# The second block's gates and recurrence inputs by seven block products, its values first and through HBM

## The chip, the cores and the metric

The kernel runs on one core of a Trainium2 chip. The core has five engines with instruction lines of their own: PE (TensorE, the matrix engine), DVE (VectorE), ACT (ScalarE), POOL (GpSimd) and SP (SyncE, which here only starts transfers). Each line is worked off in order. Operands lie in SBUF (128 partitions), matmul results in PSUM (eight banks of 128 x 512 float32), everything else in HBM. The metric is the device time of one execution in microseconds (us), the median of several runs.

## The reference: two blocks over 512 tokens

The input is 512 tokens of 2048 features, in float32. A first block (16 extra tokens, a projection to queries, keys, values and gates of two kinds of attention, an output projection) leaves its result `h`, 512 x 2048. The change is in the second block:

```
xn = rmsnorm_2(h, norm_gain)
proj = xn @ w_in                                  # 2048 -> 6 x 1024
q, k, v, g_sb, x_lru, g_lru = split(proj)
y_sb  = stick_breaking_attention(norm(q), norm(k), v) * silu(g_sb)
xc    = causal_depthwise_conv(x_lru, conv_w, conv_b)     # 4 taps
y_lru = rg_lru(xc, w_a, b_a, w_x, b_x, lam) * silu(g_lru)
h = h + concat(y_sb, y_lru) @ w_out
```

`rg_lru` is a gated recurrence along the tokens, `h_t = a_t h_{t-1} + sqrt(1 - a_t^2) (i_t x_t)`, in eight blocks of 128 channels; its gates come from small 128 x 128 products of `xc`. The gates `g_sb`, `g_lru` and the input `x_lru` are three products of 512 x 2048 by 2048 x 1024; in the kernel they are called GS, GL and XL, eight blocks of 128 columns each. The projection's 2048 input features are sixteen K tiles of 128.

## The kernel before

**Matmuls.** A float32 operand is split into two parts of a shorter format, a rounded one and the rest (`split`, lines 416 to 418: ACT rounds, DVE subtracts). A product is three passes over the parts, large by large, large by rest, rest by large; so each K tile costs three matmuls. `big` holds the split activations of all tokens, features on partitions.

**Two ways of using weights.** `fm` produces features on partitions (lhs is a weight tile, the tokens stream through: up to 512 columns). `tm` produces tokens on partitions (lhs is a tile of 128 tokens, 512 weight columns stream). Both take weight tiles of 128 x 1024 from `load_next` (SP loads to `wraw`, then a split into `wsp`, three buffers, two tiles ahead, in the order of the list `_sequence`).

**Seven products.** The first block's gates and second attention do not take the plain way. Two blocks of 128 feature columns (a pair) times two halves of the tokens times two halves of the first 12 K tiles is a 2 x 2 by 2 x 2 block product, which the function `seven` does with seven block products in place of eight, from sums of the weights and of the activations; the other 4 K tiles are plain (`rest`). The activation sums are formed once (`side_x`: `x23`, `x1s`, and a fourth one that overwrites a part of `big` when its old content is used up). The weight sums are formed for each pair: `load_raw` brings the four quarters into four slots of `wraw` (SP), `sum_up` adds further quarters to them with accumulating transfers (issued by POOL), and `produce` splits each sum into one of four slots of `wsp`. A slot is filled again as soon as its product is done: one of them holds the matrices of products 4, 3 and 7 in turn. Results are recombined by DVE from the four banks (`p1s`, `us`, `wv`, `ts`). There are 20 such pairs in the first block.

**The second block.** `side_pair` finishes `h` for a pair of token tiles: it scales, adds, stores to HBM (`h1d`), transposes on PE and splits into `big`. Then PE goes through XL (`fm`, eight blocks for each half of the tokens, 256 columns at a time), GL and GS (`fm`, 512 columns), and `tm` products for v, q and k, and the output projection (O2). The results of XL, GL and GS stay in SBUF in `ybuf`, sixteen slots. `side_lru` does the recurrence for a block once its XL is there; `sb_scores` and `sb_sums` do the eight attention heads, between q, k and O2 matmuls.

**What sets the order.** `main_work` yields after small groups of matmuls; a driver (`run`) puts steps of the side generators between them, by an estimate of when their inputs are ready. PE's order is the order of that program. The order on DVE, ACT, POOL and SP is set by `Plan`: it records every instruction, gives it a due time from the PE instructions that need it, and lists each engine's work by due time, with fixed costs per instruction and per byte of a transfer.

Of the kernel before, what the change touches and what calls it, by code (L numbers as in the profile page):

```python
# [46 lines left out]
def _units():  # L47
# [6 lines left out]
    for name, n in (("KA", 2), ("VA", 2), ("GA", 8), ("QB", 8), ("KB", 8), ("VB", 8), ("GB", 8)):  # L54
        for i in range(n):
            if name in ("KA", "VA"):
                u[(name, i)] = ("fm", 0, i, cols)
            SEVEN_COLS[(name, i)] = cols
            cols += P
# [11 lines left out]
    for name in ("GS", "XL", "GL"):  # L71
        for i in range(8):
            u[(name, i)] = ("fm", 2, i, cols)
            cols += P
# [6 lines left out]
QK_LAST = (0, 2, 3, 1)  # L81


def _pairs():

    pairs = [(("GA", i), ("GA", i + 1)) for i in range(0, 8, 2)] + [(("GB", i), ("GB", i + 1)) for i in range(0, 8, 2)]
    for h in range(0, 8, 2):
        pairs += [(("QB", h), ("KB", h)), (("VB", h), ("VB", h + 1)), (("QB", h + 1), ("KB", h + 1))]
    return pairs


PAIRS = _pairs()


def _sequence():
# [5 lines left out]
    seq += [("XL", b) for _ in range(2) for b in range(8)]  # L101
    seq += [("GL", b) for b in range(8)] + [("GS", b) for b in range(8)]
    for c in range(4):
        if c % 2 == 0:
            seq += [("v", c // 2, kg) for kg in range(4)]
        seq += [("qk", c, kg) for kg in (QK_LAST if c == 3 else range(4))]
    seq += [("O2", n, kg) for n in range(4) for kg in (0, 2, 3)] + [("O2", n, 1) for n in range(4)]
# [3 lines left out]
class Plan:  # L111
# [9 lines left out]
    def __init__(self):  # L121
        self.ins, self.engine, self.cost, self.busy, self.func, self.preds = [], [], [], [], [], []
        self.nbytes = []
# [54 lines left out]
    def __call__(self, ins):  # L178
# [50 lines left out]
        self.nbytes.append(0)  # L229
        if op == "DMACopy":  # L230
# [21 lines left out]
    def order(self):  # L252
# [36 lines left out]
        while count < N:  # L289
# [60 lines left out]
def hybrid_two_block_kernel(ctx: ExitStack, tc: tile.TileContext, wp, wq, wc, xT, xtok, par, lvec, cst, rg, pg, lruw, out):  # L350
# [183 lines left out]
    ybuf = Later(lambda: next_turn([("ybuf", [P, KT, NTOK], F32)])[0])  # L534
    ar = T([P, 6144], "ar")
# [14 lines left out]
    qd = dram.tile([NT, P, NTOK], F32, tag="qd", name="qd")  # L550

# [26 lines left out]
    taken = [0]  # L578
    barred = [seq.index((("VA", 1), 1)) + 1]
# [17 lines left out]

    def load_raw(p, r, slot):
        if p >= len(PAIRS):
# [7 lines left out]
    def sum_up(p, r, q):  # L607

        pool.dma_start(pair_raw[(p, r)], wq[p, q], accum_op=ALU.add)  # L609

    def produce(p, i):


        if p >= len(PAIRS):
# [22 lines left out]
        elif i == 6:  # L637
            w_slots[:] = [at["a"], at["d"], at["c"], at["b"]]
            load_raw(p + 1, 0, raw_slot[(p, 4)])
        elif i == 8:  # L640
            load_raw(p + 1, 1, raw_slot[(p, 5)])
            if p + 1 < len(PAIRS):
                sum_up(p + 1, 1, 2)
        elif i == 7:
            load_raw(p + 1, 2, raw_slot[(p, 2)])
        elif i == 9:
            load_raw(p + 1, 3, raw_slot[(p, 0)])
# [36 lines left out]
    def seven(p, r, c0a, c0b, evac_a1, evac_b, evac_a2, after=None):  # L684


        cs = (c0a, c0b)
        X1, X2 = slice(0, HL), slice(HL, L)

# [33 lines left out]
        produce(p + 1, 1)  # L723
# [4 lines left out]
        if p == 0:  # L728
            yield when("x4")
        yield from product(7, 1, lambda xs, j: big[:, xs, j, HL + c0b : L], slice(c0b, HL), True, False)  # L730
        produce(p + 1, 4)
# [5 lines left out]
        produce(p + 1, 2)  # L737
        yield from product(9, 3, lambda xs, j: big[:, xs, KS + j, X2], allc, False, True)
        yield from evac_a2()
        produce(p + 1, 5)  # L740
# [4 lines left out]
    def tm(units, x0, evac, kgs=range(4), toks=range(NT), before_unit=None, after_unit=None, chore=None):  # L745
# [3 lines left out]
        for i, unit in enumerate(units):  # L749
# [5 lines left out]
            if last:  # L755
# [5 lines left out]
            for n, (t, h) in enumerate(order):  # L761
                if chore and n % 2:
                    chore()
                if last:
# [9 lines left out]
                if last and n % 4 == 3:  # L774
                    yield from evac({k: accs[k] for k in (t - 1, t)})
            if after_unit:
                after_unit(kg)
        post("calm", 2500)
# [76 lines left out]
    def silu2(g_ps, rb, dst):  # L855
        g, th = et(512), et(512)
        dve.tensor_tensor(g, g_ps, rb, ALU.mult)
        ins = act.activation(th, g, AF.Tanh, scale=0.5).ins
        dve.scalar_tensor_tensor(dst, th, 1.0, g, op0=ALU.add, op1=ALU.mult)
        return ins  # L860

    def gate_y(slot, hf, o):
        y = ybuf[:, slot, hf * 256 : (hf + 1) * 256]
        dve.scalar_tensor_tensor(y, o, 0.5, y, op0=ALU.mult, op1=ALU.mult)

    def split_y(s):
        split(big[:, 0, s, :NTOK], big[:, 1, s, :NTOK], ybuf[:, s, :])
# [16 lines left out]
    def side_x():  # L884
# [26 lines left out]
        post("x4")  # L911
# [326 lines left out]
    def side_pair(p):  # L1238
# [10 lines left out]
        for i, t in enumerate(toks):  # L1249
            y = yt[:, t, :]  # L1250
            c = slice(t * P, (t + 1) * P)
            for k8 in range(2):
# [7 lines left out]
                xg = T([P, 8, P], "pt")  # L1260
                dve.tensor_tensor(xg, tp, g2[:, kts].unsqueeze(2).broadcast_to([P, 8, P]), ALU.mult)
                post("pss", 2500)
# [598 lines left out]
```

## Time and profile before

| | us |
|---|---|
| median of 3 runs (1707.7 to 1710.82) | 1708.71 |
| the profiled execution, its time | 1711.61 |
| the profiled execution, its span from first to last instruction | 1709.8 |
| PE busy | 1682.0 (98%) |
| DVE busy | 1107.2 (65%) |
| ACT busy | 900.4 (53%) |
| POOL busy | 148.8 (9%) |

Durations in the argument come from the one profiled execution; its time stands 2.9 us above the median of the runs. In the trace's stretches the first block's pairs lie about 161 to 729 us after the start, the output projection of the first block up to 929, XL up to about 1026, GL and GS up to 1213, v, q, k and the output projection with the heads from there on. A row of a group reads: line, engine, operation, tile written <- tiles read, shapes, count, busy time and mean duration of one in ns, then the engine's idle time ahead of it and what ended that.

### The profile page before, as it was taken

What the parts mean: (1) busy time and instruction counts of PE and PEld (TensorE: products, weight loads), DVE (VectorE), ACT (ScalarE), POOL (GpSimd) and SP (SyncE); (2) the same over time, 40 slices, a digit from 0 to 9 for tenths busy, and PEclk for the clock granted to TensorE, in tenths of its full rate; (3) what the DMA queues carried; (4) which work ended last, traced back from release to release, by engine and by line L of the source; (5) the groups of instructions that cost most, each with busy time, mean ns of one, the idle gap of its engine ahead of it and who ended that gap; (6) DMA issues with size and microseconds to landing.
All of it is one profiled execution on the core that took longest, in us unless ns stands there. A gap on an engine that the chain in (4) does not pass through costs nothing.

```text
span 1709.8 us, 26464 instructions
## 1 busy us (share of the span) xinstructions
PE 1682.0 (98%) x10288; PEld 1497.2 (88%) x10288; DVE 1107.2 (65%) x1861; ACT 900.4 (53%) x1493; POOL 148.8 (9%) x165
## 2 busy tenths in 40 slices
PE   8999999999999999999999999999999999999999
PEld 8779999999999999978888998888888888888887
DVE  4684697766799989883567769733223764676433
ACT  5554466664577767674454558722223654564311
POOL 0011122111212222200000001100000000000000
PEclk9999999999999999999999999999999999999999
DMA  7534767667666566553566653223323222432233
GB/s 277 188 126 126 194 157 162 163 160 163 162 136 151 135 144 137 130 189 111 190 215 235 219 186 104 87 95 99 93 92 99 75 66 95 148 112 80 81 94 128
DMA packets 85549, 239.58 MB, mean 140 GB/s; under 512 B 9632, under 2 KB 15392, under 8 KB 83744
## 3 DMA queue, kind: packets, MB, share of 16 engines
q1 hardware_dynamic: 73904, 206.43, 37.1%
q0 software_dynamic: 11520, 31.46, 11.5%
q8 instruction: 81, 1.33, 0.3%
q14 instruction: 44, 0.36, 0.1%
HBM read 220.03 MB, written 17.83 MB: 139 GB/s over the span
## 4 chain that ended last, share of the span: by engine, by line
PE 67%; DVE 4%; DMA 1%; ACT 1%; issue 1%; ACTq 0%; POOLq 0%; DVEq 0%; SPq 0%
PE pj L450 60%; PE pmt L450 2%; PE pss L450 2%; DMA wraw<-in_wq 1%; DVE wsp L418 1%; PE ptt L453 1%; PE bank L450 1%; PE pmt L453 1%; PE pss L453 1%; ACT wsp L417 1%; DVE e L1175 1%; DVE ar L1223 0%; DVE e L1191 0%; ACT e L1190 0%; DVE pt L418 0%
## 5 line engine op out<-in xcount | busy, mean ns | idle before, releaser
L450 PE MATMUL pj<-wsp,big 128*128 128x512 f32 x3072 | 734.5, 396 | 3.0 <-ACT wsp L417 1.0
L450 PEld LDWEIGHTS pj<-wsp,big 128*128 128x128 f32 x3072 | 571.7, 188 | 133.3 <-DVE big L418 1.6
L418 DVE TENSOR_TENSOR wsp<-wraw,wsp 128x1024 fp32r<-128x1024 f32 (+3 forms) x399 | 427.5, 1074 | 342.2 <-ACT wsp L417 336.2
L450 PE MATMUL pj<-big,wsp 128*128 128x264 f32 (+3 forms) x4320 | 635.3, 304 | 10.0 <-ACT wsp L417 7.2
L450 PEld LDWEIGHTS pj<-big,wsp 128*128 128x128 f32 x4320 | 582.5, 189 | 45.7 <-ACT wsp L417 7.5
L417 ACT CAST wsp<-wraw 128x1024 fp32r<-128x1024 f32 (+3 forms) x399 | 367.3, 923 | 444.5 <-PE pj L450 353.4
L609 POOL DMA_DIRECT2D wraw<-in_wq x80 | 70.3, 891 | 409.7 <-DVE wsp L418 242.0
L450 PE MATMUL pj<-x,wsp 128*128 128x264 f32 x720 | 100.8, 286 | 1.9 <-DVE wsp L418 1.9
L450 PEld LDWEIGHTS pj<-x,wsp 128*128 128x128 f32 x720 | 92.5, 188 | 3.0 <-DVE wsp L418 2.7
L417 ACT CAST pt<-ptt 128x512 fp32r<-128x512 f32 (+2 forms) x96 | 50.7, 528 | 50.0 <-PE ptt L453 48.5
L418 DVE TENSOR_TENSOR pt<-ptt,pt 128x512 fp32r<-128x512 f32 (+2 forms) x96 | 59.5, 620 | 24.5 <-ACT pt L417 24.1
L450 PE MATMUL pss<-kk,qq 128*128 128x264 f32 x448 | 72.1, 289 | 2.8 <-DVE vtail L946 1.9
L450 PE MATMUL pmt<-pt,vv 128*128 128x256 f32 (+1 forms) x528 | 69.7, 280 | 2.1 <-DVE ptail L972 2.0
L450 PEld LDWEIGHTS pmt<-pt,vv 128*128 128x128 f32 x528 | 67.1, 188 | 4.5 <-issue 2.0
L1178 ACT ACTIVATE e<-e,sm 128x528 f32<-128x528 f32 x64 | 47.1, 736 | 39.1 <-DVE sm L1175 38.9
L450 PEld LDWEIGHTS pss<-kk,qq 128*128 128x128 f32 x448 | 61.4, 188 | 5.4 <-PE ptt L453 2.6
L1383 POOL TENSOR_SCALAR_AFFINE_SELECT e<-e 128x128 f32<-128x128 f32 x32 | 12.1, 378 | 478.2 <-ACT e L1382 460.8
L453 PE MATMUL ptt<-ident,e 128*128 128x128 f32 x336 | 52.5, 273 | 0.0
L450 PE MATMUL pj<-x1s,wsp 128*128 128x264 f32 x360 | 50.1, 286 | 0.0
L1175 DVE CUSTOM_DVE_ANT_0 e<-pss,ar 128x528 f32<-128x528 f32 x64 | 44.8, 700 | 3.4 <-PE pss L450 3.3
L450 PEld LDWEIGHTS pj<-x1s,wsp 128*128 128x128 f32 x360 | 46.2, 188 | 0.2
L453 PEld LDWEIGHTS ptt<-ident,e 128*128 128x128 f32 x336 | 39.8, 140 | 2.6
(254 smaller groups left out, 1386.4 us busy)
## 6 DMA issues: line engine op xcount, KB each, us to landing
wraw<-in_wp SPq DMA_DIRECT2D x215, 512.0 KB, 3.5
wraw<-in_wq SPq DMA_DIRECT2D x80, 384.0 KB, 4.0
wraw<-in_wq POOLq DMA_DIRECT2D x80, 384.0 KB, 5.1
wraw<-in_wc SPq DMA_DIRECT2D x40, 256.0 KB, 3.2
e<-in_xT SPq DMA_DIRECT2D x28, 264.0 KB, 4.3
early<-in_xtok SPq DMA_DIRECT2D x4, 1024.0 KB, 7.8
gated<-e SPq DMA_DIRECT2D x16, 256.0 KB, 3.7
e<-yd SPq DMA_DIRECT2D x16, 256.0 KB, 4.1
```

Source lines behind the costliest of these rows:

```text
L417: act.copy(hi, src)
L418: dve.tensor_tensor(lo, src, f(hi), ALU.subtract)
L450: _queue(nc.tensor.matmul(out, lhsT, rhs, start=start, stop=stop).ins, cost)
L453: _queue(nc.tensor.transpose(out, in_, identity).ins, 110.0)
L609: pool.dma_start(pair_raw[(p, r)], wq[p, q], accum_op=ALU.add)
L1175: dve.tensor_tensor_reduce(out=halves(x), in0=s[:, :, :HL], in1=halves(bias[:, b0 : b0 + L]), scale=1.0, scalar=3e38, op0=ALU.add, op1=ALU ...
L1178: act.activation(x, x, AF.Exp, scale=-1.0, bias=nm, accum_out=l[:, m : m + 1])
L1383: pool.affine_select(z[:, t * P : w], z[:, t * P : w], [[-1, P]], ALU.is_gt, -1e30, base=0, channel_multiplier=1)
```

## The change

XL, GL and GS are computed by `seven` too, in twelve pairs of blocks, over the first 12 of the 16 K tiles, with the two halves of 256 tokens as token halves. The order is XL and GL pairs in turn, four of each, and then four GS pairs (`SECOND`).

The v products come first, ahead of the pairs: `v_half` does them for the first two token tiles as soon as these are there, and then for the other two, so each v weight tile is loaded twice, as XL's were. The values are scaled by ACT and stored to HBM (`vd`) by POOL. `side_pair` also stores the gained features of each token tile to HBM (`x2d`, POOL); `side_x2` reads them back by K tile (POOL, twelve reads) and DVE forms the operand sums. Where an accumulating transfer would add the weight quarter 2, DVE adds it (`sum_up`), so two of the four accumulating transfers of a pair are left in the second block.

The operands need the room of `ybuf`. So the gates go to HBM (`gated2`) instead; XL has two buffers (`xls`), which the convolution empties; the recurrence's result is multiplied with its gate after a load from `gated2`, and stored there. After the last pair one tile is rebuilt (`ybuf2`): GS's eight gates and the values are loaded into it, and the part of `big` that was overwritten is read again from `x2d`. The sixteen inputs of the output projection are split in a new order, the recurrence's from HBM. The first and last q, k units and O2 use the K tiles in the order 2, 3, 0, 1.

In `Plan` a transfer's price changes for all of the kernel: per byte 1/300 ns on both queues (1/260 on SP's, 1.2/260 on POOL's before), 1.9 times that if it accumulates.

```diff
-    seq += [("XL", b) for _ in range(2) for b in range(8)]
-    seq += [("GL", b) for b in range(8)] + [("GS", b) for b in range(8)]
+    seq += [("v", c, kg) for _ in range(2) for c in range(2) for kg in range(4)]
...
+    return pairs + [((name, i), (name, i + 1)) for name, i in SECOND]
+SECOND = [(name, i) for i in range(0, 8, 2) for name in ("XL", "GL")] + [("GS", i) for i in range(0, 8, 2)]
...
-                pipe = max(clock[e] + lat / 2, pipe) + self.nbytes[i] * (1.0 if e == "SP" else 1.2) / 260.0
+                pipe = max(clock[e] + lat / 2, pipe) + self.nbytes[i] * (1.9 if self.adds[i] else 1.0) / 300.0
...
     def sum_up(p, r, q):
+        if p is None:
+            return
+        if p >= NEW and q == 2:
+            dve.tensor_tensor(pair_raw[(p, r)], pair_raw[(p, r)], pair_raw[(p, 2)], ALU.add)
+            return
         pool.dma_start(pair_raw[(p, r)], wq[p, q], accum_op=ALU.add)
...
+    def side_x2():
+        yield when(("x2", 0), ("x2", 1))
+        s4 = blocks(ar[:, : KS * H2], H2)
+        def fetch(j):
+            x = et(NTOK), et(NTOK)
+            for t, kt in zip(x, (j, KS + j)):
+                pool.dma_start(blocks(t), x2d[kt // 8].rearrange("t p c -> p t c")[:, :, kt % 8 * P : (kt % 8 + 1) * P])
+            return x
+        a, b = fetch(0)
+        for j in range(KS):
+            later = fetch(j + 1) if j + 1 < KS else None
+            dve.tensor_tensor(b[:, H2:], a[:, H2:], b[:, H2:], ALU.subtract)
+            dve.tensor_tensor(a[:, H2:], a[:, H2:], a[:, :H2], ALU.subtract)
+            dve.tensor_tensor(a[:, :H2], a[:, :H2], b[:, H2:], ALU.subtract)
+            dve.tensor_tensor(s4[:, j], b[:, :H2], a[:, :H2], ALU.subtract)
+            split(x23b[:, 0, j], x23b[:, 1, j], a)
+            split(x1sb[:, 0, j], x1sb[:, 1, j], b[:, H2:])
...
+                n = min(8, 2 * KS - 8 * k8)
+                pool.dma_start(x2d[k8, t][:, : n * P], flat(xg[:, :n]))
...
-                dve.tensor_tensor_scan(ybuf[:, i, :], A(i), U(i), 0.0, ALU.mult, ALU.add)
+                dve.tensor_tensor_scan(V(i), A(i), U(i), 0.0, ALU.mult, ALU.add)
             for i in range(b - 3, b + 1):
                 yield when(("gl", i))
-                y = ybuf[:, 8 + i, :]
-                dve.scalar_tensor_tensor(y, ybuf[:, i, :], 0.5, y, op0=ALU.mult, op1=ALU.mult)
+                y = et(NTOK)
+                nc.sync.dma_start(y, gated2[8 + i])
+                dve.scalar_tensor_tensor(y, V(i), 0.5, y, op0=ALU.mult, op1=ALU.mult)
+                nc.sync.dma_start(gated2[8 + i], y)
...
+        def v_half(hf, c):
+            toks = (2 * hf, 2 * hf + 1)
+            def evac(accs):
+                yield when(("r2", hf))
+                for t in accs:
+                    x = et(NTOK)
+                    act.mul(x, accs[t], r2[:, t : t + 1])
+                    pool.dma_start(vd[t][:, c * 512 : (c + 1) * 512], x)
...
+        for k, (name, i) in enumerate(SECOND):
+            yield from pair2(name, i, k == len(SECOND) - 1)
...
+        yield when("lrudone")
+        nc.sync.dma_start(ybuf2[:, 0:8, :], gated2[0:8].rearrange("k p c -> p k c"))
+        for t in range(NT):
+            for c in range(2):
+                nc.sync.dma_start(ybuf2[:, 8 + 4 * c + t, :], vd[t][:, c * 512 : (c + 1) * 512])
```

Where instructions stand now, at three places. First PE, from the last transposes of `h` (`pss<-ident,ybuf`) on. Before:

```order
L453 MATMUL pss<-ident,ybuf 128x128 x8
L450 MATMUL pj<-big,wsp 128x256 x91
L450 MATMUL pmt<-e,ones 128x128 x2
L450 MATMUL pj<-big,wsp 128x256 x377
L450 MATMUL pss<-qq,vv 128x512 x6
L450 MATMUL pj<-big,wsp 128x256 x57
L450 MATMUL pj<-big,wsp 128x512 x14
```

And now (`y` is the pairs' operand `x23b`, `pj<-wsp,big` are v products):

```order
L454 MATMUL pss<-ident,ybuf 128x128 x8
L451 MATMUL pj<-wsp,big 128x512 x46
L451 MATMUL pmt<-e,ones 128x128 x2
L451 MATMUL pj<-wsp,big 128x512 x216
L451 MATMUL pj<-big,wsp 128x256 x18
L451 MATMUL pj<-y_10054,wsp 128x256 x18
L451 MATMUL pj<-big,wsp 128x256 x30
L451 MATMUL pj<-y_10054,wsp 128x256 x18
L451 MATMUL pj<-big,wsp 128x256 x12
L451 MATMUL pj<-x1s,wsp 128x256 x18
L451 MATMUL pj<-big,wsp 128x256 x78
```

Between the last transposes and the first product of a pair there are now 262 v matmuls; the pair's products follow with 18 matmuls each.

Second POOL, at the same place (L1227 is the end of the first block's heads, L1335 the recurrence). Before:

```order
L609 DMA wraw<-in_wq 128x768 x4
L1227 TENSOR_TENSOR ar<-ar 128x512
L1145 TENSOR_SCALAR ar<-ar 128x912
L1227 TENSOR_TENSOR ar<-ar 128x512 x2
L1335 TENSOR_TENSOR ar<-ar 128x512 x8
L1383 AFFINE_SELECT e<-e 128x128 x32
```

And now, from the store of the last token tile (`x2d<-kk`) on:

```order
L1319 DMA x2d<-kk 128x1024
L1319 DMA x2d<-kk 128x512
L945 DMA e<-x2d 128x4x128 x8
L1704 DMA vd<-e 128x512 x2
L945 DMA e<-x2d 128x4x128 x4
L1704 DMA vd<-e 128x512 x2
L625 DMA wraw<-in_wq 128x768
L1704 DMA vd<-e 128x512 x2
L625 DMA wraw<-in_wq 128x768 x5
L1391 TENSOR_TENSOR ar<-ar 128x512
L625 DMA wraw<-in_wq 128x768
```

POOL's line, which held only the recurrence's multiplications there, now holds the reads of x, the stores of v and the pairs' accumulating transfers, in one order.

Third SP, from the end of the second block's feature products on (L573 loads the weight tiles of the plain way). Before:

```order
L1308 DMA e<-in_lruw 128x256
L573 DMA wraw<-in_wp 128x1024 x2
L1308 DMA e<-in_lruw 128x256
L573 DMA wraw<-in_wp 128x1024 x64
L1728 DMA ybuf<-h1d 128x512
```

And now (L616 loads the pairs' weights, L580 those of the plain way, L1752 stores gates, L1782 reads x again):

```order
L616 DMA wraw<-in_wc 128x512 x2
L1752 DMA gated_85<-e 128x512 x2
L580 DMA wraw<-in_wp 128x1024
L1782 DMA e<-x2d 128x2x128 x6
L580 DMA wraw<-in_wp 128x1024 x5
L1752 DMA gated_85<-e 128x512 x2
L1793 DMA ybuf_13402<-gated_85 128x8x512
L1796 DMA ybuf_13402<-vd 128x512 x2
L580 DMA wraw<-in_wp 128x1024
L1796 DMA ybuf_13402<-vd 128x512 x6
L580 DMA wraw<-in_wp 128x1024 x20
```

The 64 weight tiles in a row are now preceded and split up by the reads of x, the gates and the values.

More of the change, by code (lines that the diff above doesn't have):

```diff
@@ L763, in tm @@
                     chore()
-                if last:
+                if last and stagger:
                     w = ws_[h]
@@ L777, in tm @@
                 after_unit(kg)
+        if not stagger:
+            yield from evac(accs)
         post("calm", 2500)
@@ new lines, in main_work, with free_slots, next_slot, slots @@
+        room["e"] = 4
+        todo, free = [*range(8, 16), *range(8)], set()
+        def free_slots(kg):
+            free.update(range(4 * kg, 4 * kg + 4))
+        def next_slot():
+            if todo and todo[0] in free and (todo[0] >= 8 or there(("ys", todo[0]))):
+                split_y(todo.pop(0))
+        def slots(kg):
+            while any(s in todo for s in range(4 * kg, 4 * kg + 4)):
+                if todo[0] < 8:
+                    yield when(("ys", todo[0]))
+                next_slot()
@@ L1714, in res @@
             if n < 3:
-                return ybuf[:, (8, 9, 10, 11, 12, 13, 14, 15, 0, 1, 2, 3)[n * 4 + t], :]
+                return ybuf2[:, (8, 9, 10, 11, 0, 1, 2, 3, 12, 13, 14, 15)[n * 4 + t], :]
             return ar[:, t * 512 : (t + 1) * 512]
-        late = list(range(4, 8))
-        def late_slot():
-            if late and there(("ys", late[0])):
-                split_y(late.pop(0))
         for n in range(4):
@@ L1733, in add @@
                 yield
-            yield from tm([("O2", n, kg) for kg in (0, 2, 3)], 0, add, (0, 2, 3), chore=late_slot)
-        yield when(("ys", 7))
-        while late:
-            late_slot()
+            yield from tm([("O2", n, kg) for kg in (2, 3, 0)], 0, add, (2, 3, 0), range(NT), slots, None, next_slot)
+        yield from slots(1)
         for n in range(4):
```

258 lines of the change are left out of this document (157 added, 101 removed).

## The prediction

> **What bounds the kernel now.** I read the page's engine shares and its chain of work first, then the PE groups with the shapes kept apart, and last the busy time by stretches of the span.
>
> ```profile
> span 1709.8 us, 26464 instructions
> PE 1682.0 (98%) x10288; PEld 1497.2 (88%) x10288; DVE 1107.2 (65%) x1861; ACT 900.4 (53%) x1493; POOL 148.8 (9%) x165
> ...
> GB/s 277 188 126 126 194 157 162 163 160 163 162 136 151 135 144 137 130 189 111 190 215 235 219 186 104 87 95 99 93 92 99 75 66 95 148 112 80 81 94 128
> ...
> PE 67%; DVE 4%; DMA 1%; ACT 1%; issue 1%; ACTq 0%; POOLq 0%; DVEq 0%; SPq 0%
> ```
>
> PE is busy for 98% of the span and the chain runs through it: matmul time sets the end, and every other engine matters only where it lets PE wait. So the first question is how many matmul columns leave the stream, and the second how much of that comes back as waits.
>
> ```profile
> L450 PE MATMUL pj<-wsp,big 128*128 128x512 f32 x3072 | 734.5, 396 | 3.0 <-ACT wsp L417 1.0 <-DVE big L418 1.0 <-DVE wsp L418 0.7
> L450 PE MATMUL pj<-big,wsp 128*128 128x264 f32 x2064 | 275.9, 288 | 8.6 <-ACT wsp L417 7.2 <-ACT xmisc L710 1.3
> L450 PE MATMUL pj<-big,wsp 128*128 128x512 f32 x768 | 179.3, 394 | 0.0
> ...
> L450 PE MATMUL pj<-big,wsp 128*128 128x256 f32 x768 | 92.4, 281 | 0.0
> ```
>
> Matmuls overlap, so a price is busy time by count, not the mean of one. The last two rows are exactly what the change replaces: XL (256 columns wide) at 92.4/768 = 0.1203 us each, GL and GS (512 wide) at 179.3/768 = 0.2335 us, no idle time ahead of them. The second row holds most of the first block's seven-product pairs.
>
> ```profile
> core 0: us, PE busy (x) PEld busy (x) DVE busy (x) ACT busy (x) POOL busy (x), PEclk, DMA share, GB/s
> 385.00:460.00 75.00, 72.99 (x600) 72.09 (x599) 51.01 (x93) 37.68 (x63) 10.03 (x12) 1.00 0.70 160
> 500.00:550.00 50.00, 50.00 (x417) 49.78 (x416) 47.28 (x95) 36.86 (x73) 11.14 (x10) 1.00 0.65 152
> 850.00:925.00 75.00, 73.28 (x334) 59.33 (x334) 51.60 (x71) 37.62 (x46) 0.00 (x0) 1.00 0.68 228
> 925.00:1025.00 100.00, 100.00 (x829) 98.99 (x828) 72.04 (x105) 49.95 (x56) 0.00 (x0) 1.00 0.63 202
> 1025.00:1100.00 75.00, 75.00 (x325) 60.74 (x325) 66.44 (x84) 62.87 (x83) 9.81 (x7) 1.00 0.31 95
> ...
> 1319.00:1443.00 124.00, 124.00 (x624) 103.50 (x623) 74.89 (x121) 71.76 (x138) 5.58 (x16) 1.00 0.24 77
> ```
>
> The stages to be replaced, from 925 us on, run with PE full at clock 1.00: their columns are pure path. The seven-product pairs (385 to 550) let PE wait a little where pairs follow fast, and the stage before XL (850 to 925) waits 1.72 us. The last row is four attention heads, PE full.
>
> **The saving.** XL, GL and GS go: 92.4 + 179.3 = 271.7 us. Twelve pairs come, each of seven products over 6 K tiles and four remainders over 4, three passes each: (7 x 6 + 4 x 4) x 3 = 174 matmuls of 256 columns, 2088 in all. At XL's price that is 2088 x 0.1203 = 251.2 us, a saving of 20.5 us. From above, the 264-wide row gives 275.9/2064 = 0.1337, scaled to 256 columns 0.1296: 270.7 us and almost no saving. That row is mixed with other work and with waits, and XL has the very width, so I take XL's price. The v products keep their 384 matmuls of 512 columns; attention, transposes and the recurrence keep their numbers.
>
> The Trainium skill, TensorE: Matmul & The Clock Gate, Back-to-back issue gap, speaks against halving the width: it gives about 81 ns sustained at 128 columns and 131 ns at 512. Between them 256 columns would cost, as an estimate, 98 ns, and 2088 x 98 against 768 x (98 + 131) would lose 29 us. The XL and GL rows contradict it (120 and 233 ns, a ratio of 1.94), and the measurement decides.
>
> **Waits inside the pairs.** Each pair re-splits weights into four slots (ACT rounds one half, DVE subtracts for the other). The third matrix goes into the slot of product 4 while PE does product 5 and one remainder: (18 + 12) x 0.1203 = 3.6 us.
>
> ```profile
> 424.14 0.95 DVE L418 TENSOR_TENSOR wsp<-wraw,wsp 128x768 fp32r<-128x768 f32 x1
> ...
> 425.01 0.69 DVE L1160 TENSOR_TENSOR kk<-ar,kk 64x528 fp32r<-64x528 f32 x1
> ...
> 428.50 0.83 ACT L417 CAST wsp<-wraw 128x768 fp32r<-128x768 f32 x1 [1.03 <-DMA wraw<-in_wq]
> 429.37 0.96 DVE L418 TENSOR_TENSOR wsp<-wraw,wsp 128x768 fp32r<-128x768 f32 x1 [0.93 <-ACT wsp L417]
> ...
> 430.39 1.36 PE L450 MATMUL pj<-x,wsp 128*128 128x264 f32 x9 [0.48 <-DVE wsp L418]
> ```
>
> At 428.50 ACT waited for the accumulating transfer, then came 0.83 + 0.96 us of splitting, and PE was 0.48 us too early. So 1.8 us of the 3.6 are work and 1.8 are slack for queues. The stretch 385 to 460 holds 3.1 pairs and 75.00 - 72.99 = 2.01 us of idle PE, 0.65 us a pair. The new pairs come faster (174 x 0.1203 = 20.9 us, those took 24.2), but two chained transfers a pair are gone: DVE adds matrix 2 instead.
>
> ```profile
> L418 DVE TENSOR_TENSOR wsp<-wraw,wsp 128x768 fp32r<-128x768 f32 x140 | 134.4, 961 | 52.8 <-ACT wsp L417 48.0 <-PE pj L450 4.1
> L418 DVE TENSOR_TENSOR wsp<-wraw,wsp 128x512 fp32r<-128x512 f32 x40 | 28.0, 701 | 4.0 <-ACT wsp L417 3.4 <-PE pj L450 0.3
> L720 DVE TENSOR_TENSOR xmisc<-pj,xmisc 128x264 f32<-128x264 f32 x20 | 8.6, 428 | 0.2
> L1303 DVE SCALAR_TENSOR_TENSOR e<-ybuf,prm,e 128x509 f32<-128x509 f32 x8 | 8.7, 1091 | 0.1
> L1336 DVE TENSOR_TENSOR_SCAN ybuf<-ar 128x512 f32<-128x512 f32 x8 | 9.7, 1213 | 1.2 <-POOL ar L1335 1.2
> ...
> wraw<-in_wq POOLq DMA_DIRECT2D x80, 384.0 KB, 5.1
> gated<-e SPq DMA_DIRECT2D x16, 256.0 KB, 3.7
> ```
>
> An add of 0.96 us replaces 5.1 us to landing; that pays for the pace. DVE is the engine to watch. A pair costs it 7 x 0.96 + 2 x 0.70 of splits, 2 x 0.96 of adds and 8 x 0.43 of recombining and evacuation: 13.5 us. An XL and a GL pair together add six operations of 512 columns (0.70 as the split of that size) and two blocks of recurrence, each with three convolution steps (at most 1.09), a scan (1.21) and six operations of 0.4 to 0.7: 8.2 us. Sum for two pairs: 27.0 + 4.2 + 16.4 = 47.6 us, against 41.9 us of PE and about 3 us of recurrence matmuls, 44.9. Instructions overlap a little (a 0.95 us one at 424.14, the next at 425.01), 0.08 us on each of some 64, so the load is 42.5 to 47.6 us, 95 to 106%. The stretch 500 to 550 bore DVE at 47.28 of 50 with PE at 50.00; what slips goes to the four GS pairs, which have no recurrence. SP's line now holds the gates' stores and loads between the weights; a gate's load waits for its store to land (3.7 us) and the next weights stand behind it. All this is in the price of a pair: I take the fast stretch's 0.65 us for all twelve, 7.8 us. Ends: 0 (stretch 500 to 550) and twice it, 15.7 us.
>
> **Handover from v to the pairs.** The second half of v has to hide the new operands. From the last transposes to the first product PE has 262 matmuls of 512 columns, at 734.5/3072 = 0.239 us 63 us, and weights are fetched two tiles (5.7 us) ahead: 68 us. In it move 22 weight tiles (11.5 MB), two h1 stores (2.1), for x the stores of two token tiles (1.6) and twelve reads (3.1), six v stores (1.6) and the first pair's weights (2.0): 21.9 MB.
>
> ```profile
> q1 hardware_dynamic: 73904, 206.43, 37.1%
> ...
> wraw<-in_wp SPq DMA_DIRECT2D x215, 512.0 KB, 3.5
> ...
> h1d<-ybuf SPq DMA_DIRECT2D x4, 1024.0 KB, 5.7
> ```
>
> The first queue moved 206.43 MB in 37.1% of the span, 325 GB/s while busy: 21.9 MB take 67 us, all that there is. No quoted stretch ran above 228 GB/s, where PE lost 1.72 us. DVE's work on x (six steps of about 2.8 us) stands in its line ahead of the splits of v's weights, so a late read of x delays PE's next weights; POOL has reads, v stores and the first accumulation in one line, so a v store that waits holds up the reads behind it. I take 3 us: nearest is the 1.72 us, and this is fuller. Ends: 0, and 12 us if no more than the page's best slice, 277 GB/s, comes (79 us).
>
> The Trainium skill, SBUF — State Buffer, A bandwidth-pool intuition that's wrong, gives a core about 358 GB/s from HBM. By that the same bytes take, as an estimate, 61 us, and this term would be 0; no run here shows such a rate.
>
> **Handover to q and k.** Behind the last pair SP issues 4.2 MB of gates and values among weight tiles that PE uses up in 24 x 0.239 = 5.7 us each. A tile behind the first 2.6 MB needs 8.1 us at 325 GB/s, 3.5 to land and 2.4 of splitting (1.8 x 1024/768) against 11.5 us of lead: 2.5 us late; ends 0 and 5. The values themselves are wanted with the first head, 267 matmuls later. The heads now follow without the v matmuls between the fourth and fifth, at the spacing that the last stretch above hid with DVE at 75 of 124 us under q, k and output matmuls: nothing; if that cover broke, a head's exposed step of 1 to 2 us each. The planner's transfer prices changed too and with them the order of DVE, ACT and SP in the first block, not PE's: nothing, +-1 us.
>
> **Sum.** 1709.8 - 20.5 + 7.8 + 3 + 2.5 = 1702.6 us of span. The runs' median, 1708.71, is 1.1 below the profiled span (that execution took 1711.61): 1701.5 us.
>
> **Rivals.** (a) All is hidden, as now from 925 us on: 1688 to 1690. For it: PE full beside DVE at 95% from 500 to 550. Against: the waits from 385 to 460. (b) Slower: the slot that is filled three times a pair. Two re-splits a pair (products 3 and 7) have 3.6 us and need 1.8; with ACT loading a table and DVE at its limit each comes 1.1 us late: 24 x 1.1 = 26 us, with the handovers 1720. It decides from (20.5 - 5.5)/24 = 0.63 us each; the one shown was 0.48. (c) Transfers stay at 277 GB/s in v's second half: 12 us there with 7.8 and 2.5, about 1710, no change. (d) 256 columns cost what the mixed 264 row says, waits included: 1708 and 5.5 for the handovers, 1713. The page's width rule would be this one gone further (29 us lost, about 1738 as an estimate); the XL row leaves it no chance of its own.
>
> **Chances.** Forecast (1694 to 1706) 0.52; (a) 0.2; (b) 0.12; (c) 0.11; (d) 0.05. A measurement tells 0.2%, 3.4 us, from no change. Faster: (a) and nearly all of the forecast, 0.7; same 0.15; slower 0.15. The range reaches from (a) past (c): 1688 to 1714.
>
> **What would show it.** Right: 2088 matmuls of 256 columns at about 0.12 us; idle PE of 0.3 to 1 us a pair, released by ACT or DVE on wsp; some idle PE near the first pair, with transfers near 300 GB/s. Wrong: over 1.5 us idle a pair, an operand of the first pair that is many us late, or heads that wait near the end.

## The result, and the profile after

| | us |
|---|---|
| kernel before, median of 6 runs (1707.7 to 1712.55) | 1709.76 |
| changed kernel, median of 6 runs (1718.98 to 1724.87) | 1720.41 |
| ratio, 95% interval | 1.0064 (1.0049 to 1.008) |
| span of the profiled execution, before and after | 1709.8 and 1717.4 |

The change makes the kernel 0.64% slower. The forecast was 1701.5 with a range of 1688 to 1714: wrong in sign, and the time lies outside the range. From the page of the changed kernel:

```profile
span 1717.4 us, 28307 instructions
PE 1668.4 (97%) x10840; PEld 1512.0 (88%) x10840; DVE 1207.1 (70%) x2073; ACT 945.4 (55%) x1581; POOL 188.2 (11%) x217
...
L451 PE MATMUL pj<-wsp,big 128*128 128x512 f32 x3072 | 745.6, 400 | 23.9 <-ACT wsp L418 18.3
```

PE is busy for 13.6 us less than before (1682.0), yet the span is 7.6 us longer: PE idles for 49.0 us where it idled for 27.8. The last row says where. The plain products of 512 columns waited 23.9 us, against 3.0 before, 18.3 of it for the rounded halves of weights. Next the busy time by stretches: last transposes, second half of v (three rows), pairs.

```profile
core 0: us, PE busy (x) PEld busy (x) DVE busy (x) ACT busy (x) POOL busy (x), PEclk, DMA share, GB/s
936.00:967.50 31.50, 31.50 (x156) 26.00 (x155) 26.44 (x36) 19.39 (x20) 4.79 (x8) 1.00 0.89 313
967.50:985.00 17.50, 10.53 (x37) 7.75 (x36) 6.83 (x16) 5.95 (x11) 3.73 (x5) 0.82 0.41 129
985.00:1005.00 20.00, 15.11 (x51) 11.15 (x51) 9.92 (x15) 5.32 (x7) 3.43 (x6) 0.82 0.67 205
1005.00:1025.00 20.00, 13.80 (x51) 9.81 (x50) 11.13 (x17) 8.18 (x12) 2.63 (x4) 0.83 0.46 130
...
1044.40:1308.00 263.60, 259.23 (x2137) 256.26 (x2135) 222.45 (x346) 157.33 (x221) 32.04 (x33) 1.00 0.64 170
```

From 967.5 to 1025 us everything is slack at once: PE, DVE, ACT, and the transfers (129 to 205 GB/s, at 41 to 67% of the DMA engines' time). That is no lack of bandwidth: right before, PE was full while 313 GB/s moved. And the granted clock falls to 0.82. On PE's own line in that place:

```profile
967.54 5.79 PE L451 MATMUL pj<-wsp,big 128*128 128x512 f32 x24
980.11 1.22 PE L451 MATMUL pj<-wsp,big 128*128 128x512 f32 x2 [6.78 <-ACT wsp L418]
981.53 10.04 PE L451 MATMUL pj<-wsp,big 128*128 128x512 f32 x34 [0.19 <-DVE wsp L419]
996.23 1.22 PE L451 MATMUL pj<-wsp,big 128*128 128x512 f32 x2 [4.67 <-ACT wsp L418]
...
1015.82 1.22 PE L451 MATMUL pj<-wsp,big 128*128 128x512 f32 x2 [5.27 <-ACT wsp L418]
1017.27 27.30 PE L451 MATMUL pj<-wsp,big 128*128 128x512 f32 x112 [0.23 <-DVE wsp L419]
1044.40 2.32 PE L451 MATMUL pj<-big,wsp 128*128 128x256 f32 x18
```

These 216 matmuls take 76.9 us (967.54 to 1044.40). At 0.2335 us each they need 50.4, so 26.4 us are lost: 18.1 as idle PE (16.7 in the three long waits, 1.4 in short ones) and the rest, 8.3, as slower matmuls, most of them right behind the three long waits: 34 take 10.04 us there (0.295 each) where the last 112 take 27.30 (0.244).

What ends the first of these waits can be followed on the other engines' lines (all engines, 973 to 980 us):

```profile
973.21 0.75 POOL L945 DMA_DIRECT2D e<-x2d  x1 [2.81 <-issue]
976.69 0.42 DVE L951 TENSOR_TENSOR e<-e 128x256 f32<-128x256 f32 x1 [6.38 <-DMA e<-x2d]
976.92 0.76 POOL L945 DMA_DIRECT2D e<-x2d  x1 [2.96 <-issue]
...
977.15 0.41 ACT L418 CAST x1s<-e 128x256 fp32r<-128x256 f32 x1 [6.86 <-DVE e L951]
...
979.02 1.04 ACT L418 CAST wsp<-wraw 128x1024 fp32r<-128x1024 f32 x1
```

Read it upwards, from PE's start at 980.11. PE waits for the rounding of a v weight tile (979.02). That weight stands on ACT's line behind the rounding of `x1s`, an operand of the pairs, which waits for DVE's first step on it (976.69), which waits for a read of `x2d` to land. The weight tile has nothing to do with that read; it only stands behind it. And that read was issued late: it went at 973.21 after 2.81 us in which POOL stood idle, and the next one at 976.92 after another 2.96, though an issue takes only 0.75 us. The waits of the stretch 960 to 1048, by total (us, times, longest):

```profile
ACT x1s L418 <- DVE e L951: 32.0, 6, 7.9
POOL e L945 <- issue: 29.2, 8, 5.9
DVE e L951 <- DMA e<-x2d: 26.5, 6, 6.4
...
PE pj L451 <- ACT wsp L418: 16.7, 3, 6.8
```

The chain is plain, and its root is "issue": POOL waits 29.2 us for nothing that the profile names. So the first question for experiments was what holds POOL between two reads. Each read takes 128 partitions of four pieces of 512 bytes, 512 contiguous pieces in all; no other transfer that POOL issues in this kernel has more than 128.

### The profile page after: what moved, and what is told of

The parts are those of the page before. It is cut to its first block, busy times and chain, and to the rows that moved or that the text cites. A ratio compares the mean times of both kernels' runs of the same rounds, so it can differ in the third digit from the quotient of the medians.

```text
span 1717.4 us, 28307 instructions
## 1 busy us (share of the span) xinstructions
PE 1668.4 (97%) x10840; PEld 1512.0 (88%) x10840; DVE 1207.1 (70%) x2073; ACT 945.4 (55%) x1581; POOL 188.2 (11%) x217
## 4 chain that ended last, share of the span: by engine, by line
PE 63%; DVE 5%; DMA 3%; issue 3%; ACT 2%; POOL 0%; SPq 0%; DVEq 0%; ACTq 0%; POOLq 0%
PE pj L451 56%; PE pmt L451 2%; PE pss L451 2%; DVE wsp L419 2%; DMA wraw<-in_wp 1%; PE ptt L454 1%; DMA wraw<-in_wq 1%; PE bank L451 1%; ACT wsp L418 1%; PE pmt L454 1%; DMA e<-x2d 0%; DMA vd<-e 0%; PE pss L454 0%; DVE ar L1276 0%; POOL e L945 0%
## 5 line engine op out<-in xcount | busy, mean ns | idle before, releaser
L451 PE MATMUL pj<-wsp,big 128*128 128x512 f32 x3072 | 745.6, 400 | 23.9 <-ACT wsp L418 18.3
L451 PEld LDWEIGHTS pj<-wsp,big 128*128 128x128 f32 x3072 | 575.7, 190 | 159.1 <-ACT wsp L418 20.6
L419 DVE TENSOR_TENSOR wsp<-wraw,wsp 128x768 fp32r<-128x768 f32 (+3 forms) x459 | 464.1, 1016 | 231.7 <-ACT wsp L418 224.5
L418 ACT CAST wsp<-wraw 128x768 fp32r<-128x768 f32 (+3 forms) x459 | 401.6, 878 | 385.8 <-PE pj L451 291.3
L451 PE MATMUL pj<-big,wsp 128*128 128x264 f32 (+2 forms) x4224 | 539.2, 283 | 10.6 <-ACT wsp L418 7.2
L451 PEld LDWEIGHTS pj<-big,wsp 128*128 128x128 f32 x4224 | 518.6, 189 | 13.6 <-ACT wsp L418 7.5
L625 POOL DMA_DIRECT2D wraw<-in_wq x104 | 90.8, 883 | 631.1 <-DVE wsp L419 496.4
L451 PE MATMUL pj<-x1s,wsp 128*128 128x264 f32 (+1 forms) x576 | 78.0, 285 | 1.9 <-DVE e L1760 1.9
L451 PEld LDWEIGHTS pj<-x1s,wsp 128*128 128x128 f32 x576 | 72.9, 188 | 2.2 <-DVE e L1760 2.1
L451 PE MATMUL pj<-y,wsp 128*128 128x256 f32 x432 | 55.6, 282 | 0.0
L451 PEld LDWEIGHTS pj<-y,wsp 128*128 128x128 f32 x432 | 53.4, 189 | 0.0
```

The lines of the kernel that those rows point to most:

```text
L418: act.copy(hi, src)
L419: dve.tensor_tensor(lo, src, f(hi), ALU.subtract)
L451: _queue(nc.tensor.matmul(out, lhsT, rhs, start=start, stop=stop).ins, cost)
```

## The experiments

Two theories. **POOL's line** (theory P): a read of 512 pieces blocks POOL for 3.7 us (the time of the pieces), DVE's and ACT's lines stand behind the reads, PE behind them. **Bandwidth** (theory B): the second half of v has too much to move, as the prediction's term had it. A third question (theory O) is how much is owed to the planner, which takes these reads as quick and so places the work on x ahead of weights that PE needs sooner.

### The reads on SP's line

```diff
-                pool.dma_start(blocks(t), x2d[kt // 8].rearrange(...)[...])
+                nc.sync.dma_start(blocks(t), x2d[kt // 8].rearrange(...)[...])
```

> One edit: the twelve reads of x (128 partitions x 4 pieces of 512 bytes each) are issued by SP and not by POOL; bytes, layout and work are the same. Theory P (POOL needs about 3.7 us to write out the 512 pieces of one read, so the reads come one by one and late, and the lines of DVE and ACT, where a step on x stands ahead of the splits of v's weights, hold PE back): the 26.7 us lost between the last transposes and the first pair (18.1 us of idle PE and the half clock that follows it) fall to under 6, time about 1698. Theory B (transfers are short of bandwidth there, the prediction's rival): the same bytes move, so PE still loses 15 us or more, time above 1710.

1695.05 us median (1693.21 to 1700.58), ratio to before 0.991 (0.9882 to 0.9938). One word turns the loss into a gain. PE's line and the stretches, in the trace of this kernel:

```profile
969.06 6.25 PE L451 MATMUL pj<-wsp,big 128*128 128x512 f32 x26
976.17 5.84 PE L451 MATMUL pj<-wsp,big 128*128 128x512 f32 x24 [0.85 <-DVE wsp L419]
982.24 38.74 PE L451 MATMUL pj<-wsp,big 128*128 128x512 f32 x166 [0.23 <-DVE wsp L419]
1020.82 2.32 PE L451 MATMUL pj<-big,wsp 128*128 128x256 f32 x18
```

```profile
958.00:980.00 22.00, 21.15 (x95) 16.90 (x94) 17.19 (x27) 12.11 (x17) 1.63 (x3) 1.00 0.83 280
980.00:1000.00 20.00, 19.77 (x86) 15.72 (x85) 16.82 (x27) 12.23 (x16) 0.55 (x1) 1.00 0.89 282
```

The 216 matmuls take 51.8 us (969.06 to 1020.82) in place of 76.9, with 1.1 us of idle PE and the clock at 1.00. The same bytes move, at 280 GB/s, and SP issues the first two reads within 0.93 us. Bandwidth as the cause is out.

### The features stored by K tile, the reads on POOL in 128 pieces of 2 KB

```diff
-    x2d = dram.tile([2, NT, P, 1024], F32, tag="x2d", name="x2d")
+    x2d = dram.tile([2 * KS, P, NTOK], F32, tag="x2d", name="x2d")
...
-                pool.dma_start(blocks(t), x2d[kt // 8].rearrange(...)[...])
+                pool.dma_start(t, x2d[kt])
...
-                pool.dma_start(x2d[k8, t][:, : n * P], flat(xg[:, :n]))
+                nc.sync.dma_start(x2d[8 * k8 : 8 * k8 + n, :, t * P : (t + 1) * P].rearrange("k p c -> p k c"), xg[:, :n])
```

> x is stored to HBM by K tile (in pieces of 512 bytes, issued by SP), so that each of the twelve reads, still on POOL, is 128 whole rows of 2 KB: same bytes, a quarter of the pieces. Theory P: POOL needs about 0.6 to 0.9 us for a read, as for its other transfers of 128 rows, the loss falls to under 6 us, time about 1698. If not the pieces but POOL's line or its queue as such were slow: no change, above 1712. Theory B: no change.

1695.21 us (1691.28 to 1698.79), ratio 0.9901 (0.9875 to 0.9927). POOL's line now:

```profile
960.09 0.55 POOL L945 DMA_DIRECT2D e<-x2d  x1 [7.05 <-PE pss L454]
960.81 1.69 POOL L945 DMA_DIRECT2D e<-x2d  x3 [0.17 <-issue]
```

Four reads are issued in 2.4 us, the pairs start at 1024.74, and the last 216 v matmuls take 54.7 us. The edit also moves the stores of x from POOL to SP, in pieces of 512 bytes; they are no rival, since in the changed kernel POOL's last store of x goes at 958.34 and the reads still stand 3.65 us apart at 1009. So it is neither POOL's line nor the pieces alone: POOL with whole rows is quick, and SP with 512 pieces is quick.

### The reads on POOL in 256 pieces of 1 KB

```diff
-    x2d = dram.tile([2, NT, P, 1024], F32, tag="x2d", name="x2d")
+    x2d = dram.tile([2 * KS, 2, P, NTOK // 2], F32, tag="x2d", name="x2d")
...
+                pool.dma_start(blocks(t, NTOK // 2), x2d[kt].rearrange("h p c -> p h c"))
...
+                nc.sync.dma_start(x2d[8 * k8 : 8 * k8 + n, t // 2, :, t % 2 * P : (t % 2 + 1) * P].rearrange("k p c -> p k c"), xg[:, :n])
```

> The changed kernel with reads on POOL as they are, but in 256 pieces of 1 KB (the features stored by K tile and token half). Theory P (a transfer issued by POOL holds POOL's line for a time that grows with its number of pieces): about half of the 3.7 us that 512 pieces took, 1.8 to 2.1 us from one read to the next, twelve reads in some 24 us instead of 51; that is within what PE has there, so 1695 to 1698 us. Rival (there is a fixed price for any read whose rows are not contiguous): again 3.7 us a read and 1710 to 1720 us.

1696.27 us (1692.29 to 1700.32), ratio 0.9909 (0.9887 to 0.9931). The time came as expected, but neither mechanism did. POOL's line, and the read of 957.17 by itself:

```profile
957.17 2.19 POOL L945 DMA_DIRECT2D e<-x2d  x3 [7.25 <-issue]
961.93 0.72 POOL L945 DMA_DIRECT2D e<-x2d  x1 [2.57 <-issue]
```

```profile
L945 POOL DMA_DIRECT2D e<-x2d x1: 727/727/727, 957.2 to 957.2; - x1
...
DMA to landing us min/median/max: 4.4/4.4/4.4
```

Three reads go out back to back, 0.73 us each, and not 1.8 to 2.1. The fourth waits, and it starts at 961.93, right after the first has landed (957.17 + 4.4 = 961.6). The same comes again at 981.12: three reads, the first lands after 4.2 us (985.3), and the fourth goes at 985.69. Now the changed kernel's own reads with the same eyes, all twelve and the one of 973.21:

```profile
L945 POOL DMA_DIRECT2D e<-x2d x12: 749/758/775, 959.2 to 1009.9; - x12
...
DMA to landing us min/median/max: 3.3/3.4/6.4
...
L945 POOL DMA_DIRECT2D e<-x2d x1: 749/749/749, 973.2 to 973.2; - x1
...
DMA to landing us min/median/max: 3.4/3.4/3.4
```

973.21 + 3.4 = 976.6, and the next starts at 976.92. With 512 pieces there is always just one read under way, and the next one goes 0.3 us after it has landed; with 256 pieces there are three. Both sizes fit one reading: POOL's queue has room for at least 768 pieces that have not landed yet and for fewer than 1024, and an issue that finds no room waits. So the first theory was right about the place and wrong about the price. POOL does not need 3.7 us for 512 pieces. It needs 0.76, and then the reads go one at a time at the pace of their landing, 3.3 to 6.4 us. In the changed kernel two stores of 128 rows go at 988.62 right behind a read of 512 pieces, 768 in all, which fits too. Bytes don't fit: four whole-row reads of the same 256 KB went together above. That the room is counted in pieces is worked out from these cases; nothing in the profile names it. The Trainium skill, Perfetto Trace Analysis, DMA Instruction — SWDGE (GPSIMD), says that for transfers of this queue the profile's end is the last descriptor written and not the data moved, and speaks of a descriptor buffer that can be too small for a transfer; the rows agree (an issue of 0.76 us, a landing at 3.4), and the page gives no size.

### The same reads, but the planner knows their price

```diff
             cost, busy = (1300.0 + nb / 260.0, 60.0) if e == "SP" else (3300.0 + nb / 220.0, 870.0)
+            if e != "SP":
+                busy = max(870.0, 7.2 * max(nb / 4 / ap.ap[-1][1] for g in aps for ap in g))
```

> One edit, in the planner alone: a transfer on POOL's line is priced at 7.2 ns for each contiguous piece that it names (a read of x 3.7 us in place of 0.87). No instruction changes, only the order on the lines of DVE, ACT and SP; the reads are as slow as before. Theory P in its strict form (the reads are simply too slow): 12 x 3.7 = 44 us of reads remain, part of the loss stays, 8 us or more. Theory O (it is not the slowness but the order: the planner takes a read for quick and puts the step on x ahead of weight splits that PE needs sooner; 63 us of v would hold 44 us of reads): the loss falls to under 6 us, time about 1698. Theory B: no change, above 1712.

1713.62 us (1708.77 to 1716.92), ratio 1.0012 (0.9999 to 1.0025): no difference to before, some 7 us below the changed kernel. The reads are as slow as they were (first at 963.0, last at 1017.1), but DVE and ACT have their work on x further back (line numbers of this kernel are two higher):

```profile
974.24 26.64 PE L453 MATMUL pj<-wsp,big 128*128 128x512 f32 x112 [0.53 <-DVE wsp L421]
1003.20 0.74 PE L453 MATMUL pj<-wsp,big 128*128 128x512 f32 x2 [2.32 <-ACT wsp L420]
...
1025.32 1.00 PE L453 MATMUL pj<-wsp,big 128*128 128x512 f32 x2 [3.69 <-ACT wsp L420]
```

Up to 1000 us PE runs nearly through, and the longest wait is 3.69 us where it was 6.78. There was room to do so: in the changed kernel the last step on x was done by 1018 us, and the first product that reads these operands starts at 1046.6. A planner that knows the price takes back about half of the stretch's loss: the 216 matmuls take 64.5 us, 971.33 to 1035.80, so 14.1 us are lost in place of 26.4. As expected of the strict theory P, 8 us or more stay while the reads are late; the order alone (theory O) does not cure it. The gain of the whole kernel is smaller. The last transposes come at 959.43 here and at 955.64 in the changed kernel; the edit raises the planner's price of every POOL transfer, to 922 ns for those of 128 pieces where it was 870, and whether that is the reason was not tested.

### The planner's old transfer prices, and the new ones alone

The change also brought new transfer prices, which the prediction took as worth nothing. First the changed kernel with the old ones:

```diff
-                pipe = max(clock[e] + lat / 2, pipe) + self.nbytes[i] * (1.9 if self.adds[i] else 1.0) / 300.0
+                pipe = max(clock[e] + lat / 2, pipe) + self.nbytes[i] * (1.0 if e == "SP" else 1.2) / 260.0
```

> The change with the planner's old transfer prices (1/260 ns a byte on SP, 1.2/260 on POOL, no surcharge for accumulating). In the changed kernel the first block's pairs began 6.1 us sooner than before and the last transposes came 4.5 us sooner, with the same PE order. If that is the prices' work (order of DVE, ACT and SP alone), the first block loses those 4 to 6 us again, time about 1722 to 1727; if it is chance of one run, time as the changed kernel's within 2 us. The loss ahead of the pairs should stay at 20 us or more either way.

1729.68 us (1726.34 to 1732.62), ratio 1.0102 (1.008 to 1.0125), 9.3 us above the changed kernel and more than the 1722 to 1727 that was expected. The loss ahead of the pairs stays, as expected: the 216 matmuls take 74.7 us. The new prices help the changed kernel, and not only in the second block: the last transposes come at 962.63 with the old prices and at 955.64 with the new. So the kernel before got the new prices and nothing else (the reverse of the two lines above):

> The kernel before, with nothing changed but the two transfer prices in the planner (1/300 ns per byte, 1.9 times that if it accumulates). The prediction priced them at nothing, plus or minus 1 us. The changed kernel's pairs begin 6.1 us earlier than the old ones and its last transposes come 4.5 us earlier (955.6 against 960.1), and the changed kernel with the old prices lost 9 us. Theory A (the gain up to the last transposes comes from these prices alone): 1704 to 1706 us, 4 to 6 below the kernel before, first pair operand at about 166 to 168 instead of 172.7. Theory B (the new prices help only together with the other new work, which loads SP and POOL in another way): 1708 to 1711, no difference.

1706.48 us (1705.58 to 1706.8), with before at 1711.27 beside it: ratio 0.9967 (0.9954 to 0.9981), faster by 5.6 us by the ratio and 4.8 by the medians. That fits theory A, if a little short of its 1704 to 1706; in the first block's first pair the product on `x1s` starts at 167.48 in place of 172.73, as expected. PE's line at the last transposes, in the trace of before and of this kernel:

```profile
960.13 1.03 PE L453 MATMUL pss<-ident,ybuf 128*128 128x128 f32 x8
```

```profile
954.11 1.04 PE L454 MATMUL pss<-ident,ybuf 128*128 128x128 f32 x8
```

Between these two traces the prices are worth 6.0 us up to there. A single trace tells this point to some 2 us: in the changed kernel and the five with mended reads, all with the new prices, it lies between 953.8 and 958.1. The changed kernel thus carries a gain that has nothing to do with its seven products; without it the rest of the change costs 1% (1.0102 measured with the old prices, 1.0064/0.9967 = 1.0097 by division).

### Both mends together, and the values' stores off POOL

The features by K tile and the reads on SP; then also the eight stores of the values:

```diff
-                pool.dma_start(t, x2d[kt])
+                nc.sync.dma_start(t, x2d[kt])
```

> The changed kernel with the features stored by K tile (so that a read is 128 rows of 2 KB) and the twelve reads issued by SP. It joins the two mends that each gave about 1695 us. If the reads' price on POOL's line was the whole of the loss, either mend takes all of it and the two together give the same again: 1692 to 1696, first pair at about 1021, idle PE in the last 216 v matmuls 1 to 2 us. If the 512-byte pieces also cost something on SP's line or in the DMA engines, it is 2 to 3 us faster than with the reads on SP alone: 1690 to 1692.

1694.93 us (1694.19 to 1700.19), ratio 0.9908 (0.9889 to 0.9927): the same as with either mend alone, as expected. The pairs start at 1020.75, but PE idles for 2.9 us in the last 216 v matmuls, where 1 to 2 were expected. Two stretches of its trace, and PE's line in the second, hold something for later:

```profile
936.00:954.50 18.50, 18.50 (x93) 15.31 (x92) 17.42 (x29) 13.33 (x15) 1.17 (x2) 1.00 1.01 358
965.00:985.00 20.00, 17.12 (x68) 13.29 (x68) 14.96 (x27) 11.03 (x16) 1.08 (x2) 0.91 0.93 324
```

```profile
969.63 0.73 PE L451 MATMUL pj<-wsp,big 128*128 128x512 f32 x2 [2.35 <-ACT wsp L418]
```

The first row has PE full at 358 GB/s. In the second, one long wait of 2.35 us is left, and the mean granted clock of the stretch falls to 0.91: the clock's records have half speed from 971.9 to 975.3.

```diff
-                    pool.dma_start(vd[t][:, c * 512 : (c + 1) * 512], x)
+                    nc.sync.dma_start(vd[t][:, c * 512 : (c + 1) * 512], x)
```

> As the one with rows of 2 KB read by SP, and the eight stores of the values issued by SP too, so that POOL issues nothing in v's second half but the first accumulation. The prediction said that a v store that waits on POOL's line holds up what stands behind it. If such a store still costs anything, this is 1 us or more faster than with the stores on POOL; if not, the same within 0.2%, or slower by up to 2 us, since SP's line then holds stores that wait for ACT ahead of weight loads.

1696.09 us (1692.54 to 1697.28), ratio 0.9901 (0.9883 to 0.9919): the same. No cost of the values' stores on POOL's line shows once the reads are not held there; the runs would tell some 3 us.

The fastest version is thus the change with its reads mended, in any of the three ways, at about 1695 us: 0.9% faster than before and 1.5% faster than the changed kernel. Against the kernel before with the new prices (1706.48), which leaves the planner's part out, it is 10 to 11 us faster. Whether DVE's add of quarter 2 or an accumulating transfer is the cheaper one in the second block stays open: the latter was not tried.

## Why the prediction was wrong

**The step that failed: the handover from v to the pairs.** It was put at 3 us, with ends of 0 and 12. It is 26.4 us (76.9 - 50.4), and alone it turns the forecast over: with the 1.4 us that this stretch loses when the reads are on SP (51.8 - 50.4), the kernel lies in the forecast's own range of 1694 to 1706 (1695.05). Some 5 us of that come from the planner's prices, which the sum had at nothing; without them it would be about 1700, an estimate, and still in that range. The reasoning failed at its unit. The step counted bytes, 21.9 MB against 68 us, and took the queue's rate as the limit. Bytes were never the limit: 313 GB/s passed with PE full right before, and 358 in a later run. The trace of before could have told it. Of the stretches that the prediction quoted none ran above 228 GB/s, and it said that no run here showed 358; but this stretch of the same trace has 371 with PE full:

```profile
12.00:30.00 18.00, 18.00 (x138) 18.00 (x138) 12.01 (x17) 9.86 (x14) 0.00 (x0) 1.00 0.97 371
```

The limit was one read under way at a time, 12 reads in 51 us (959.2 to 1009.9), and no row of the trace of before showed a POOL transfer of that many pieces, so its price ought to have been bounded from both sides. I gave the reads a size in bytes and none in pieces. The prediction did name how it would hurt ("a late read of x delays PE's next weights", "POOL has reads, v stores and the first accumulation in one line"), and that is the chain in the trace; but the price came from another mechanism. A bound was at hand: twelve reads one after the other, at the 5.1 us to landing that its own quoted row had for POOL's transfers, are 61 us of the 68, with the work on x behind the last one. That should have been a rival of its own, and it was the one that came.

**The clock.** That matmuls also run slower behind a wait was not in the sum. Of the 26.4 us it is most of the 8.3 that are not idle time. The rows with PEclk 0.82 show it, and the 34 matmuls in 10.04 us. The clock's records have three stretches of 6.8 us at half speed, from 978.6, 995.7 and 1012.8 on. Each begins inside one of the waits of 6.78, 4.67 and 5.27 us and outlasts it; some 15 us of busy PE lie in them, about 7 us lost. The Trainium skill, TensorE: Matmul & The Clock Gate, What's actually happening, says that the array drops to half speed after an idle window of about 3.4 us and comes back after a busy one as long. The records agree on the half; the matmuls of 512 columns start 0.427 us apart from 982.1 to 985.1 and 0.232 where nothing waits, a factor of 1.84. On the lengths the trace differs: 6.8 us and not 3.4 at half speed, and in the kernel with both mends a wait of 2.35 us, shorter than the page's window, brought one of 3.4. The estimate by the page, one window of 3.4 us at half speed and so 1.7 us lost for each long wait, would be 5 us in place of some 7.

**The saving** was nearly right: 20.5 us were forecast, and 23.0 came. A pair without recurrence products takes 20.6 us from one start of its `x1s` product to the next (the last two in the trace of the changed kernel):

```profile
1277.93 2.32 PE L451 MATMUL pj<-x1s,wsp 128*128 128x256 f32 x18
...
1298.52 2.32 PE L451 MATMUL pj<-x1s,wsp 128*128 128x256 f32 x18
```

Twelve are 247.1 us. From one start to the next, the kernel before took 5.76 us for 48 matmuls of 256 columns and 9.96 for 43 of 512 (PE's line in its trace):

```profile
947.85 5.92 PE L450 MATMUL pj<-big,wsp 128*128 128x256 f32 x48
953.61 1.04 PE L453 MATMUL pss<-ident,ybuf 128*128 128x128 f32 x8
...
1029.59 10.12 PE L450 MATMUL pj<-big,wsp 128*128 128x512 f32 x43
1039.55 1.56 PE L450 MATMUL pss<-qq,vv 128*128 128x512 f32 x6
```

768 of each are 92.2 + 177.9 = 270.1 us, so 23.0 us are saved. Rival (d), dearer narrow products, is out.

**Waits inside the pairs** were put at 7.8 us. The last row of the table by stretches has 263.60 - 259.23 = 4.4, and the waits of PE in that stretch are three:

```profile
PE pj L451 <- DVE wsp L419: 2.4, 2, 1.6
PE pj L451 <- DVE e L1760: 1.9, 1, 1.9
```

The last one is for DVE to empty a PSUM bank into a result's buffer (L1760). Late weights, which rival (b) put at 1.1 us twice a pair, come to 2.4 us for all twelve. DVE, "the engine to watch" at 95 to 106% while XL and GL run, was at 88% (148.19 of 167.6 us):

```profile
1044.40:1212.00 167.60, 166.75 (x1373) 164.93 (x1372) 148.19 (x231) 105.97 (x150) 21.96 (x23) 1.00 0.63 164
```

**Handover to q and k**: 2.5 forecast; 0.22 + 0.77 = 1.0 us of idle PE at 1308 us. **The heads** without v between them: PE is full from 1326 to 1450 us, as forecast. **The planner's prices**: "nothing, +-1 us" forecast, 4.5 us in place (the last transposes at 955.64 against 960.13, single traces) and about 5 us alone in the kernel before. That PE's order stays the same was taken as a reason; but the prices move DVE's, ACT's and SP's lines, and with them the waits.

The sum by its own terms: -4.5 (first block) - 23.0 (saving) + 26.4 (v to pairs) + 4.4 (pairs) + 1.0 (q and k) = +4.3 us; the spans differ by 7.6. The other 3 us lie in no single place, and were not followed further.

## What to carry to other kernels

Price a transfer by its pieces and by how many of them its queue can have under way, not by its bytes alone: a strided read of 512 pieces on POOL's queue went one at a time, while the same read on SP, or the same bytes in fewer pieces, cost PE 1 to 5 us in that stretch and not 26. Where engines work off fixed lines, a late operand delays whatever stands behind it, needed or not; so a planner must know the true price of each new kind of transfer, or put its consumers last. When a small shared cost is changed along with a large edit, test it alone: here it was worth 0.3% of the kernel before and 0.5% of the changed one, and would have been credited to the edit.

## What was not expected of the hardware

- A POOL transfer of 512 pieces of 512 bytes is issued in 0.76 us, but the next one goes only when it has landed (about 0.3 us later in ten of eleven cases; a landing takes 3.3 to 6.4 us); of 256 pieces three go together, and of 128 four went in 2.4 us. SP issues the 512-piece reads without such a stop, two in 0.93 us.
- A wait of 2.35 to 6.78 us brought 3.4 to 6.8 us at half speed, by the clock records of these traces; the part of them that lies inside the wait costs nothing more.
- 371 GB/s over 18 us with PE full in the kernel before, where only loads run, and 358 over 18.5 us in the one with both mends, with the DMA engines' share at 0.97 and 1.01. The Trainium skill, SBUF — State Buffer, A bandwidth-pool intuition that's wrong, has about 358 GB/s for one core from HBM; the first stretch lies above it.
